# First model of a two-model kernel: conv and rope on VectorE alone, another order of gates, attention and output product

## The chip, the cores and the metric

The kernel runs on one core of a Trainium2 chip. The metric is the device time of one execution in microseconds. Engines are named as in the profile: PE is TensorE's matmul, PEld its weight load, DVE is VectorE, ACT is ScalarE, POOL is GpSimd, SP is SyncE (which here only issues DMAs).

## The reference

Two models of depth 2 run one after the other on 256 tokens of width 1024, all in float32; the change touches only the first. One layer of the first model is, cut to what matters:

```python
n = rmsnorm(h, norm_g[i])
z = n @ w_in[i] + b_in[i]
(c_val, c_glu, c_gate, p_in, p_gate, q, k, v, a_gate, qi, ki, wi) = jnp.split(z, cut, axis=-1)
ya = conv_module(c_val, c_glu, ...) * silu(c_gate)       # 256 channels
yb = pool_mixer(p_in, ...) * silu(p_gate)                # 256 channels
q, k, qi, ki = rope(q), rope(k), rope(qi), rope(ki)
yc = sparse_attention(q, k, v, qi, ki, wi) * silu(a_gate)  # 512 channels
h = h + concatenate([ya, yb, yc], axis=-1) @ w_out[i]
h = h + (p[i] @ ple_w[i]) * sigmoid(h @ ple_gate_w[i])
```

`conv_module` multiplies `val * sigmoid(glu)`, convolves each channel over time with 31 taps (causal, depthwise), then layernorm, silu and a 256 x 256 product. `rope` rotates halves of each head. `sparse_attention` scores all keys with a small indexer (`qi`, `ki`, `wi`), keeps the 64 best per query, and runs softmax attention of 8 heads over those.

## The kernel before

**Layout and tiles.** Activations lie with channels on partitions and the 256 tokens along the free axis. A weight *unit* is 128 x 1024 float32 (512 KB): one output tile of 128 columns with 8 blocks of 128 rows. `rawunit` (L421, its transfer L425) loads it on SP's queue into one of 4 buffers `raw`; `unit` (L431) splits it into a high half `hl[:, 0]` on ACT (L437) and a low half `hl[:, 1]` on DVE (L445), 4 buffers. `mtile` (L542) multiplies one tile: 8 blocks, each three products (`mm3`, L384 to L386: high x high, high x low, low x high) into a PSUM bank `mm`. A few first tiles use the unsplit weights (`ftile`).

**Stages of `layer1` (L716).** In source order: value and glu tiles of the convolution; the key-index tile `ki`, with rope; the token-major tiles `pin` (pooling input and index weights); 2 query-index tiles `qi`, with rope; 4 tiles `q` and 4 tiles `k`, each group with rope; 4 units of `v`; 8 gate tiles `sil`; the output product in two halves of 8 tiles, each over 4 blocks of the concatenation `cat` (`xx[:, 0]`); then the per-layer embedding. `cat` holds convolution in blocks 0 and 1, pooling in 2 and 3, the four head pairs of attention in 4 to 7. The first half of the output product contracts blocks 0 to 3, the second 4 to 7.

**Other work in between.** The convolution (`conv1`), the indexer (`index1`), pooling (`pool1`) and attention (`attn1`) are generators in a list `tasks`. After each tile `tick` (L463) runs tasks with a budget of 1500: it takes the first task that does something, and subtracts the cost that its `yield` names. `add(..., front=True)` puts a task first. With `turns` set, each task that was tried goes to the end of the list. `until` runs tasks up to a named result, `flush` runs all to their end. A task that lacks an input yields `None`. In the first layer the matrix for the second model's modulation is also computed in small pieces (`ada`, `wada` transfers), one piece per tick. The tasks set the source order; the compiler then orders each engine's queue itself, by dependencies and source order, so that an instruction may run well ahead of work written before it.

**The convolution (L927).** For channel block `j` of 2, `acc[:, j]` starts as tap 0 times the input `u` (L931) and takes 30 more taps (`taps`, L934). Those of `j = 0` are one DVE instruction each (`stt`, L392). With `CONV_POOL = 1` those of `j = 1` are all two instructions: ACT scales the input into `zh` (one of 2 buffers, L405), and GpSimd adds it to `acc` (L943). The task of `j = 1` is put first with cost 200 for two taps, the other has 800. Then follow the layernorm, silu, the product `pw` and the gate (from L954 on), which need the value tiles to be done (`late`). The output product begins when `conv` and `pool` are done (L871, L872); all tasks are flushed before its second half.

**Rope (L695).** For two tiles at a time: a shuffle on DVE into `ropes` (L704), two products with cosine and sine (L707, L708) and a sum (L709), each 128 x 512. With `ROPE = 'qk'` the latter three are on GpSimd for `q` and `k`, which makes 12 per layer, and on DVE for `qi` and `ki`.

**Attention (L1051).** Eight steps (4 head pairs x 2 query blocks): two score products, mask and maximum on DVE (`aL`, L1067), exponential on ACT, transposes and value products on PE, then the gate and the split into `cat`. It is put last in the list, behind convolution and pooling, and begins when the masks `imk` are there.

**Order of the gates.** `GATES` names which gate each of the 8 gate tiles is; it also orders weights and biases on the host.

Of the kernel before, what the change touches and what calls it, by code (L numbers as in the profile page):

```python
# [24 lines left out]
DOWN_PACE = 2.5  # L25
CONV_POOL = 1
CONVP = 200
CONVY = 800
INNER = 500
# [20 lines left out]
PINR = True  # L50
ROPE = 'qk'
ROPEB = 2
# [43 lines left out]
def head_cols(base, heads):  # L96
# [4 lines left out]
    0, 256, 512, 768, 1024, 1280, 1792, 2304, 2816, 3328, 3584, 3648)  # L101
GATES = [("c", 0), ("c", 1), ("a", 0), ("p", 0), ("p", 1), ("a", 1), ("a", 2), ("a", 3)]
B1_TILES = (
# [15 lines left out]
def block1_units(i, a):  # L119
    w = a["w_in"][i]  # L120
    u = [fm(w, c) for c in B1_TILES[:5]]
    u += tm(w, TOKC, 3)
    u += [fm(w, c) for c in B1_TILES[5:15]]
    u += tm(w, rng(V, 512), 2)
    u += [fm(w, c) for c in B1_TILES[15:]]
    wo = a["w_out"][i]
    u += [np.concatenate([fm(wo[g * 512 : g * 512 + 512], rng(m * 128, 128)) for m in (m0, m0 + 1)], 1)
          for g in range(2) for m0 in range(0, 8, 2)]
    pw = a["ple_w"][i]
    u += [np.concatenate([fm(pw, rng(m * 128, 128)) for m in range(g * 4, g * 4 + 4)], 1) for g in range(2)]  # L130
    gw = a["ple_gate_w"][i]
    u += [fm(gw, rng(m * 128, 128)) for m in range(8)]
    return u
# [216 lines left out]
class Prog:  # L350
# [191 lines left out]
    def mtile(s, c0, n, unit=None, ks=range(KT), off=0):  # L542
        hl = unit if unit is not None else s.unit()
        ps = s.bank("mm")
        ks = list(ks)
        for k in ks:
            o = (k + off) * 128
            w = [hl[:, e, o : o + 128] for e in range(2)]
# [167 lines left out]
    def layer1(s, i):  # L716
# [104 lines left out]
        for nme in ("q", "k"):  # L821
            raw = s.t([128, 4, T], nme + "r", 1)
            for j in range(4):
                ps = wtile()
                s.a(raw[:, j], ps[:, :T], AF.Identity, bias=bias()[0])
                s.tick()
            s.rope(raw, 4, nc.gpsimd if nme in ROPE else None)
            qk.append(raw)
# [16 lines left out]
        if i == 0:  # L845
            s.pin(nc.scalar.dma_start(s.x2[:, :, :T], A["ctxT"].rearrange("p (k t) -> p k t", k=KT)))
        s.add(s.attn1(qk[0], qk[1], v, cat, st8))
        s.pace = PACE[2]
# [21 lines left out]
        s.pool_share = 0.0  # L870
        s.until(st8, "conv")  # L871
        s.until(st8, "pool")  # L872


        for g in range(2):
            if g:
                s.flush()
            for m in range(KT):
                if m % 2 == 0:
                    hl = s.unit()  # L880
                ps = s.mtile(0, T, hl, range(4 * g, 4 * g + 4), m % 2 * 4 - 4 * g)
                s.tt(h[:, m], h[:, m], ps[:, :T], ALU.add)
                if g:
                    s.split(s.xx[:, 1, 0, m], s.xx[:, 1, 1, m], h[:, m])
                s.tick()
# [41 lines left out]
    def conv1(s, i, P, H, u, cat, st8):  # L927
        nc = s.nc
        acc = s.t([128, 2, T], "acc", 1)
        for j in range(2):  # L930
            s.ts(acc[:, j], u[:, j, 0:T], P["dw"][:, j * CONV_K : j * CONV_K + 1], ALU.mult,  # L931
                 P["dwb"][:, j : j + 1], ALU.add)

        def taps(j, cost):  # L934
            for k in range(1, CONV_K):
                w = P["dw"][:, j * CONV_K + k : j * CONV_K + k + 1]
                x = u[:, j, k : k + T]
                if j == 0 or k < CONV_POOL:
                    s.stt(acc[:, j], x, w, acc[:, j], ALU.mult, ALU.add)
                else:  # L940
                    pr = s.t([128, T], "zh", 2)
                    s.a(pr, x, AF.Copy, scale=w)
                    nc.gpsimd.tensor_tensor(acc[:, j], acc[:, j], pr, ALU.add)  # L943
                if k % 2 == 0:
                    yield cost
            st8["taps", j] = True

        s.add(taps(1, CONVP), front=True)
        yield from taps(0, CONVY)
        while ("taps", 1) not in st8:  # L950
            yield None
        while "late" not in st8:
# [98 lines left out]
    def attn1(s, q, k, v, cat, st8):  # L1051
# [22 lines left out]
        for n, (pr, qt) in enumerate(steps):  # L1074
# [38 lines left out]
            s.tt(yc, po[:, :T], st8["a", pr], ALU.mult)  # L1113
            s.split(cat[0][:, 4 + pr], cat[1][:, 4 + pr], yc)
            yield 700

# [635 lines left out]
```

## Time and profile before

| | |
|---|---|
| median of 3 runs | 1469.65 us (1467.91 to 1471.45) |
| profiled execution | 1469.05 us, its span 1467.2 us |
| instructions | 25799 |
| granted clock, mean | 0.979 of full speed |
| busy: PE | 1403.8 us |
| busy: DVE | 1057.1 us |
| busy: ACT | 695.6 us |
| busy: POOL | 160.3 us |
| moved by DMA | 218.02 MB |

The first model takes the first 430 us or so of the span: its first layer up to about 230 us, its second from there. In a profile's row the engine, line and operation stand first, then the tile written and those read (`out<-in`), shapes, the count, busy time and mean duration. Busy time counts overlapping instructions once; a duration can be longer than the time from one start to the next, since an engine begins an instruction before the record of the one ahead has ended. The granted clock is TensorE's, as a share of 2.4 GHz; its other level is 1.2 GHz, and a share in between is a mean over a stretch.

### The profile page before, as it was taken

The numbers are of one execution on the slowest core, as the hardware profiler recorded it, in microseconds if no ns is written. First come the engines' busy times: TensorE is split into PE (matmuls) and PEld (weight loads), VectorE is DVE, ScalarE is ACT, GpSimd is POOL, SyncE is SP. The second block draws the span as 40 slices with busy tenths as digits, with TensorE's granted clock in tenths as the row PEclk, the third lists the DMA queues.
The fourth block names the chain that finished last, engine by engine and source line by source line (L and its number), as shares of the span: only waits on it lengthen the run. The fifth ranks groups of instructions, "written<-read, shape, count | busy, mean of one in ns | idle before, by whom it ended". The sixth has DMA issues, their size and how long they took to land.

```text
span 1467.2 us, 25799 instructions
## 1 busy us (share of the span) xinstructions
PE 1403.8 (96%) x10178; PEld 1196.6 (82%) x10178; DVE 1057.1 (72%) x2128; ACT 695.6 (47%) x1294; POOL 160.3 (11%) x176
## 2 busy tenths in 40 slices
PE   8889999689999999999999999999999999999997
PEld 7657688677997877768888888888898887999997
DVE  6895656996976655465898886787367665698694
ACT  4635655636765233454444422343246245476562
POOL 1840001920020000002100000000210000100001
PEclk9999999999999999999999999999999999999998
DMA  7677685343452211112353565555333233376662
GB/s 263 249 254 263 206 310 187 101 144 115 135 172 86 88 59 55 58 55 101 89 183 117 164 223 201 171 186 174 89 97 101 87 97 92 108 211 195 185 197 77
DMA packets 63761, 218.02 MB, mean 149 GB/s; under 512 B 7254, under 2 KB 12312, under 8 KB 63512
## 3 DMA queue, kind: packets, MB, share of 16 engines
q1 hardware_dynamic: 58224, 208.17, 44.7%
q10 hardware_dynamic: 5416, 8.20, 1.8%
q8 instruction: 80, 1.31, 0.4%
q14 instruction: 41, 0.34, 0.1%
HBM read 215.30 MB, written 1.05 MB: 147 GB/s over the span
## 4 chain that ended last, share of the span: by engine, by line
PE 79%; DVE 9%; POOL 4%; issue 3%; ACT 3%; DMA 2%; ACTq 0%; POOLq 0%; DVEq 0%; SPq 0%
PE mm L384 21%; PE mm L385 21%; PE mm L386 21%; PE ax L381 10%; DVE hl L445 3%; POOL acc L943 2%; PE mm L381 2%; PE ada L381 2%; DMA raw<-in_units_dram 1%; DVE acc L392 1%; PE ax L1705 1%; ACT hl L437 1%; POOL sqa L526 1%; DVE isc L392 1%; DVE xx L392 1%
## 5 line engine op out<-in xcount | busy, mean ns | idle before, releaser
L384 PE MATMUL mm<-xx,hl 128*128 128x256 f32 (+1 forms) x1720 | 557.9, 326 | 16.2 <-ACT qr L405 7.6
L386 PE MATMUL mm<-xx,hl 128*128 128x256 f32 (+1 forms) x1720 | 549.0, 320 | 4.9 <-DVE hl L445 4.9
L385 PE MATMUL mm<-xx,hl 128*128 128x256 f32 (+1 forms) x1720 | 549.7, 320 | 0.0
L445 DVE TENSOR_TENSOR hl<-raw,hl 128x1024 fp32r<-128x1024 f32 x286 | 359.2, 1256 | 107.4 <-ACT hl L437 104.2
L437 ACT ACTIVATE hl<-raw 128x1024 fp32r<-128x1024 f32 x286 | 301.0, 1054 | 172.9 <-PE mm L386 151.3
L384 PEld LDWEIGHTS mm<-xx,hl 128*128 128x128 f32 x1720 | 328.4, 191 | 60.5 <-issue 13.1
L386 PEld LDWEIGHTS mm<-xx,hl 128*128 128x128 f32 x1720 | 328.7, 191 | 32.2 <-DVE hl L445 6.3
L385 PEld LDWEIGHTS mm<-xx,hl 128*128 128x128 f32 x1720 | 328.9, 192 | 29.7 <-issue 6.3
L392 DVE SCALAR_TENSOR_TENSOR y<-mm,sp,y 128x255 f32<-128x255 f32 (+1 forms) x184 | 109.1, 595 | 25.8 <-ACT y L405 24.3
L384 PE MATMUL mm<-hid,hl 128*128 128x256 f32 (+1 forms) x374 | 123.0, 329 | 0.0
L385 PE MATMUL mm<-hid,hl 128*128 128x256 f32 (+1 forms) x374 | 123.0, 329 | 0.0
L386 PE MATMUL mm<-hid,hl 128*128 128x256 f32 (+1 forms) x374 | 122.7, 328 | 0.0
L405 ACT ACTIVATE y<-mm,sp 128x256 f32<-128x256 f32 (+1 forms) x92 | 60.4, 657 | 116.2 <-PE mm L386 116.0
L526 POOL TENSOR_TENSOR sqa<-sqa,sq 128x256 f32<-128x256 f32 x36 | 32.1, 896 | 690.5 <-ACT sq L405 689.8
L384 PEld LDWEIGHTS mm<-hid,hl 128*128 128x128 f32 x374 | 70.5, 188 | 7.2
L385 PEld LDWEIGHTS mm<-hid,hl 128*128 128x128 f32 x374 | 70.5, 188 | 7.1
L386 PEld LDWEIGHTS mm<-hid,hl 128*128 128x128 f32 x374 | 70.5, 188 | 6.9
L392 DVE SCALAR_TENSOR_TENSOR x<-mm,mod,x 128x256 f32<-128x256 f32 x96 | 43.5, 478 | 44.2 <-PE mm L386 44.0
L385 PE MATMUL mm<-hl,xx 128*128 128x416 f32 (+3 forms) x192 | 68.4, 356 | 5.2 <-DVE hl L445 5.2
L664 DVE CUSTOM_DVE_ANT_0 wada<-wada,crow,sp 128x1024 f32<-128x1024 f32 x48 | 61.0, 1280 | 11.1 <-DMA wada<-in_wadaT_dram 10.8
L384 PE MATMUL mm<-hl,xx 128*128 128x416 f32 (+3 forms) x192 | 68.1, 356 | 0.4 <-DVE glr L1306 0.2
L386 PE MATMUL mm<-hl,xx 128*128 128x416 f32 (+3 forms) x192 | 67.1, 350 | 0.0
(279 smaller groups left out, 1752.1 us busy)
## 6 DMA issues: line engine op xcount, KB each, us to landing
raw<-in_units_dram SPq DMA_DIRECT2D x296, 512.0 KB, 3.7
wada<-in_wada_dram SPq DMA_DIRECT2D x48, 512.0 KB, 4.9
wada<-in_wadaT_dram SPq DMA_DIRECT2D x48, 512.0 KB, 4.6
nab<-in_nab_dram ACTq DMA_DIRECT2D x12, 192.0 KB, 2.5
x<-in_xT_dram SPq DMA_DIRECT2D x4, 256.0 KB, 5.2
x<-in_ctxT_dram ACTq DMA_DIRECT2D x1, 1024.0 KB, 6.6
crow<-in_crow_dram SPq DMA_DIRECT2D x1, 1024.0 KB, 6.6
c<-in_c_dram ACTq DMA_DIRECT2D x1, 928.0 KB, 5.2
```

Source lines behind the costliest of these rows:

```text
L381: return s.nc.tensor.matmul(out, lhsT, rhs, start=start, stop=stop, **kw)
L384: s.nc.tensor.matmul(out, l[0], r[0], start=start, stop=False)
L385: s.nc.tensor.matmul(out, l[0], r[1], start=False, stop=False)
L386: s.nc.tensor.matmul(out, l[1], r[0], start=False, stop=stop)
L392: s.nc.vector.scalar_tensor_tensor(out, a, sc, b, op0, op1)
L405: s.nc.scalar.activation(out, in_, func, bias=bias, scale=scale)
L437: a = nc.scalar.activation(hl[:, 0], raw, AF.Copy)
L445: b = nc.vector.tensor_sub(hl[:, 1], raw, hl[:, 0].bitcast(F32))
L526: (eng or s.nc.vector).tensor_tensor(st["acc"], st["acc"], sq, ALU.add)
L664: nc.vector.tensor_tensor_reduce(out=out, in0=w, in1=c[:, j], scale=1.0, scalar=bias[:, m : m + 1], op0=ALU.mult, op1=ALU.add, accum_out=m ...
L943: nc.gpsimd.tensor_tensor(acc[:, j], acc[:, j], pr, ALU.add)
L1705: nc.tensor.transpose(pt[:, kt * 128 : kt * 128 + 128], L[j][:, kt * 128 : kt * 128 + 128], s.ident)
```

## The change

It touches the first model only, in six places. (1) All 60 convolution taps of a layer are DVE instructions, both channel blocks in turn, with a cost of 900 for each two; no tap is on ACT and GpSimd. (2) All rope work is on DVE. (3) Attention is put first in the task list, and from there up to the second half of the output product the tasks take turns. (4) The gate tiles come in the order pooling 0, attention 0, pooling 1, attention 1 to 3, convolution 0 and 1. (5) The output product contracts blocks 2 to 5 (pooling and the first two head pairs) in its first half and 6, 7, 0, 1 (the other head pairs and the convolution) in its second; the rows of `w_out` are put in that order on the host, and `mtile` counts blocks of the unit by position. (6) The first half waits for pooling and the second head pair, no longer for the convolution, which only the flush before the second half waits for.

```diff
--- before.py
+++ after.py
@@ -23,9 +23,7 @@
 FIRST = 2
 PAIR_PACE = 1.7
 DOWN_PACE = 2.5
-CONV_POOL = 1
-CONVP = 200
-CONVY = 800
+CONVY = 900
 INNER = 500
 INNER_K = (3,)
 R_TICK, NQ_TICK, SC_TICK = 1500, 2500, 3000
@@ -48,7 +46,7 @@
 PRE = 0
 WARM2 = (3, 3, 3)
 PINR = True
-ROPE = 'qk'
+
 ROPEB = 2
 START = (0, 0)
 RAW0 = (0, 2)
@@ -99,7 +97,10 @@
 
 C_VAL, C_GLU, C_GATE, P_IN, P_GATE, Q, K, V, A_GATE, QI, KI, WI = (
     0, 256, 512, 768, 1024, 1280, 1792, 2304, 2816, 3328, 3584, 3648)
-GATES = [("c", 0), ("c", 1), ("a", 0), ("p", 0), ("p", 1), ("a", 1), ("a", 2), ("a", 3)]
+GATES = [("p", 0), ("a", 0), ("p", 1), ("a", 1), ("a", 2), ("a", 3), ("c", 0), ("c", 1)]
+
+
+WO_ORDER = (2, 3, 4, 5, 6, 7, 0, 1)
 B1_TILES = (
     [rng(C_VAL, 128), rng(C_VAL + 128, 128), rng(C_GLU, 128), rng(C_GLU + 128, 128)]
     + [head_cols(KI, [0]) + head_cols(KI, [0])]
@@ -123,7 +124,7 @@
     u += [fm(w, c) for c in B1_TILES[5:15]]
     u += tm(w, rng(V, 512), 2)
     u += [fm(w, c) for c in B1_TILES[15:]]
-    wo = a["w_out"][i]
+    wo = np.concatenate([a["w_out"][i][k * 128 : k * 128 + 128] for k in WO_ORDER])
     u += [np.concatenate([fm(wo[g * 512 : g * 512 + 512], rng(m * 128, 128)) for m in (m0, m0 + 1)], 1)
           for g in range(2) for m0 in range(0, 8, 2)]
     pw = a["ple_w"][i]
@@ -543,8 +544,8 @@
         hl = unit if unit is not None else s.unit()
         ps = s.bank("mm")
         ks = list(ks)
-        for k in ks:
-            o = (k + off) * 128
+        for q, k in enumerate(ks):
+            o = (q + off) * 128
             w = [hl[:, e, o : o + 128] for e in range(2)]
             s.mm3(ps[:, :n], w, [s.mv(e, k, c0, n) for e in range(2)], k == ks[0], k == ks[-1])
             if s.inner and k in INNER_K:
@@ -824,7 +825,7 @@
                 ps = wtile()
                 s.a(raw[:, j], ps[:, :T], AF.Identity, bias=bias()[0])
                 s.tick()
-            s.rope(raw, 4, nc.gpsimd if nme in ROPE else None)
+            s.rope(raw, 4)
             qk.append(raw)
 
         s.pool_share = SHARE[1]
@@ -844,7 +845,8 @@
         st8["late"] = True
         if i == 0:
             s.pin(nc.scalar.dma_start(s.x2[:, :, :T], A["ctxT"].rearrange("p (k t) -> p k t", k=KT)))
-        s.add(s.attn1(qk[0], qk[1], v, cat, st8))
+        s.add(s.attn1(qk[0], qk[1], v, cat, st8), front=True)
+        s.turns = True
         s.pace = PACE[2]
         sil = s.t([128, 8, T], "sil", 1)
         if i == DEPTH - 1:
@@ -868,17 +870,18 @@
             s.tick()
         s.pace = PACE[3]
         s.pool_share = 0.0
-        s.until(st8, "conv")
         s.until(st8, "pool")
+        s.until(st8, ("att", 1))
 
 
         for g in range(2):
             if g:
+                s.turns = False
                 s.flush()
             for m in range(KT):
                 if m % 2 == 0:
                     hl = s.unit()
-                ps = s.mtile(0, T, hl, range(4 * g, 4 * g + 4), m % 2 * 4 - 4 * g)
+                ps = s.mtile(0, T, hl, WO_ORDER[4 * g : 4 * g + 4], m % 2 * 4)
                 s.tt(h[:, m], h[:, m], ps[:, :T], ALU.add)
                 if g:
                     s.split(s.xx[:, 1, 0, m], s.xx[:, 1, 1, m], h[:, m])
@@ -930,25 +933,11 @@
         for j in range(2):
             s.ts(acc[:, j], u[:, j, 0:T], P["dw"][:, j * CONV_K : j * CONV_K + 1], ALU.mult,
                  P["dwb"][:, j : j + 1], ALU.add)
-
-        def taps(j, cost):
-            for k in range(1, CONV_K):
-                w = P["dw"][:, j * CONV_K + k : j * CONV_K + k + 1]
-                x = u[:, j, k : k + T]
-                if j == 0 or k < CONV_POOL:
-                    s.stt(acc[:, j], x, w, acc[:, j], ALU.mult, ALU.add)
-                else:
-                    pr = s.t([128, T], "zh", 2)
-                    s.a(pr, x, AF.Copy, scale=w)
-                    nc.gpsimd.tensor_tensor(acc[:, j], acc[:, j], pr, ALU.add)
-                if k % 2 == 0:
-                    yield cost
-            st8["taps", j] = True
-
-        s.add(taps(1, CONVP), front=True)
-        yield from taps(0, CONVY)
-        while ("taps", 1) not in st8:
-            yield None
+        for k in range(1, CONV_K):
+            for j in range(2):
+                s.stt(acc[:, j], u[:, j, k : k + T], P["dw"][:, j * CONV_K + k : j * CONV_K + k + 1], acc[:, j],
+                      ALU.mult, ALU.add)
+            yield CONVY
         while "late" not in st8:
             yield None
         o256 = s.t([128, 128], "o256", 1)
@@ -1112,6 +1101,7 @@
             yc = s.t([128, T], "yc", 2)
             s.tt(yc, po[:, :T], st8["a", pr], ALU.mult)
             s.split(cat[0][:, 4 + pr], cat[1][:, 4 + pr], yc)
+            st8["att", pr] = True
             yield 700
```

## Rows read from the trace of the kernel before

**Rows 1.** Head of the page.

```profile
span 1467.2 us, 25799 instructions
```

**Rows 2.** Windows: width; busy PE, PEld, DVE, ACT, POOL (count); clock, DMA, GB/s.

```profile
24.00:107.00 83.00, 68.98 (x497) 54.88 (x496) 77.09 (x140) 43.64 (x78) 50.26 (x43) 0.94 0.74 254
107.00:195.00 88.00, 86.54 (x746) 65.41 (x747) 54.28 (x142) 46.16 (x106) 0.82 (x1) 1.00 0.74 249
244.00:322.00 78.00, 60.95 (x410) 55.38 (x409) 74.01 (x127) 41.16 (x72) 48.81 (x42) 0.91 0.45 138
322.00:391.00 69.00, 68.22 (x533) 58.70 (x532) 55.71 (x144) 46.17 (x107) 1.59 (x2) 1.00 0.40 124
730.00:780.00 50.00, 50.00 (x216) 40.36 (x215) 47.06 (x70) 20.07 (x28) 0.00 (x0) 1.00 0.54 165
```

**Rows 3.** Waits of PE, 24 to 107 us: total us, times, longest.

```profile
PE ada L381 <- ACT adae L405: 5.3, 1, 5.3
PE mm L386 <- DVE hl L445: 4.9, 5, 2.1
```

**Rows 4.** Waits of PE, 244 to 322 us.

```profile
PE mm L384 <- ACT qr L405: 7.6, 3, 4.4
PE mm L385 <- DVE hl L445: 4.0, 1, 4.0
```

**Rows 5.** DVE groups, 24 to 107 us: busy us, mean ns | idle before.

```profile
L445 DVE TENSOR_TENSOR hl<-raw,hl 128x1024 fp32r<-128x1024 f32 x19 | 27.2, 1438 | 4.7 <-ACT hl L437 4.7
L392 DVE SCALAR_TENSOR_TENSOR acc<-u,sp,acc 128x256 f32<-128x256 f32 x30 | 23.9, 797 | 0.5
...
L392 DVE SCALAR_TENSOR_TENSOR isc<-irl,pin,isc 128x256 f32<-128x256 f32 x3 | 2.2, 740 | 0.0
L1041 DVE MAX8 im<-iwk 128x8 f32<-128x128 f32 x7 | 2.0, 279 | 0.0
...
L707 DVE TENSOR_TENSOR qi<-qi,c 128x512 f32<-128x512 f32 x1 | 1.2, 1242 | 0.0
```

**Rows 6.** DVE groups, 244 to 322 us.

```profile
L445 DVE TENSOR_TENSOR hl<-raw,hl 128x1024 fp32r<-128x1024 f32 x19 | 28.3, 1489 | 2.2 <-ACT hl L437 2.2
L392 DVE SCALAR_TENSOR_TENSOR acc<-u,sp,acc 128x256 f32<-128x256 f32 x28 | 23.4, 835 | 0.2
```

**Rows 7.** DVE groups, 322 to 391 us.

```profile
L445 DVE TENSOR_TENSOR hl<-raw,hl 128x1024 fp32r<-128x1024 f32 x17 | 20.7, 1217 | 0.1
...
L392 DVE SCALAR_TENSOR_TENSOR acc<-u,sp,acc 128x256 f32<-128x256 f32 x2 | 1.0, 478 | 0.0
...
L401 DVE TENSOR_TENSOR v<-mm,tokb 128x512 f32<-128x512 f32 x1 | 0.7, 669 | 0.0
```

**Rows 8.** POOL groups, 24 to 107 us.

```profile
L943 POOL TENSOR_TENSOR acc<-acc,zh 128x256 f32<-128x256 f32 x30 | 30.4, 1012 | 18.9 <-ACT zh L405 17.0
L708 POOL TENSOR_TENSOR ropes<-ropes,c 128x512 f32<-128x512 f32 x4 | 7.5, 1864 | 0.0
```

**Rows 9.** An ACT group, 24 to 107 us.

```profile
L405 ACT ACTIVATE zh<-u,sp 128x256 f32<-128x256 f32 x30 | 14.8, 505 | 14.2 <-POOL acc L943 14.2
```

**Rows 10.** Tile acc, first layer: ns min/median/max, first and last start us.

```profile
L392 DVE SCALAR_TENSOR_TENSOR acc<-u,sp,acc x30: 459/835/1518, 26.8 to 89.6; 128x256 f32<-128x256 f32 x30
```

**Rows 11.** DVE in order of time, first layer: start us, duration us.

```profile
81.36 0.47 DVE L392 SCALAR_TENSOR_TENSOR acc<-u,sp,acc 128x256 f32<-128x256 f32 x1
81.75 0.28 DVE L1041 MAX8 im<-iwk 128x8 f32<-128x128 f32 x1
...
105.58 0.29 DVE L398 TENSOR_SCALAR imk<-imk 128x256 f32<-128x256 f32 x1
```

**Rows 12.** DVE in order of time, second layer.

```profile
327.46 0.48 DVE L392 SCALAR_TENSOR_TENSOR acc<-u,sp,acc 128x256 f32<-128x256 f32 x1
...
344.88 0.43 DVE L411 TENSOR_TENSOR xx<-acc,xx 128x256 fp32r<-128x256 f32 x1 [0.36 <-ACT xx L410]
```

**Rows 13.** Tile aL, both layers: first and last start us.

```profile
L1067 DVE CUSTOM_DVE_ANT_0 aL<-ax,imk x32: 270/348/425, 145.0 to 371.8; 128x128 f32<-128x128 f32 x16, 128x256 f32<-128x256 f32 x16
```

## The prediction

> **What bounds the kernel now.** I read the page's head, then busy times by stretch, then the waits of PE, then VectorE (DVE) group by group. The profiled execution spans 1467.2 us [rows 1] and took 1469.05 us, 0.6 us under the median of the three runs, 1469.65; I make the sum on 1469.05 and add the 0.6. PE carries the kernel, but not evenly [rows 2]. In 24 to 107 us (first layer, from the key-index tile to the value tiles) it is busy 68.98 of 83 us at a clock of 0.94, and in 244 to 322 us (the same part of the second layer) 60.95 of 78 us at 0.91. In the stretches behind each (gates, attention, output product) it idles 1.5 and 0.8 us at full clock. So this change can win at most what is lost in two stretches, which I call A and B. In A that is 14.0 us idle and 68.98 x 0.06 = 4.1 us of clock: floor 64.8 us. In B it is 17.1 us and 60.95 x 0.09 = 5.5 us: floor 55.5 us.
>
> What PE waits for there is named in [rows 3, 4]: the low halves of weights (`hl` on DVE, 4.9 us in A, 4.0 in B), the copy `adae` (5.3 us) and the copies `qr` (7.6 us), both on ACT. The reader should look one step further back. DVE is busy 77.09 of 83 us in A and 74.01 of 78 in B [rows 2], so it is the engine behind `hl`. ACT is not full (43.64 us), but its queue is in order, and 30 scaled copies `zh` for GpSimd's convolution taps stand in it and sat 14.2 us waiting for GpSimd [rows 9]; what is queued behind them, `hl` high halves and the copies that free PE's banks, waits with them.
>
> Now the point on which all rests. DVE's 77 us are not 77 us of work. In A the same instruction costs more than behind B, where GpSimd does nearly nothing: a tap 797 ns against 478, a low half 1438 against 1217, an index sum 740 against a tap's 478, a rope product of 512 columns 1242 against 669 for the addition of that width [rows 5, 7]. MAX8, with one input, takes 279 ns between them [rows 5]. GpSimd's own taps take 1012 ns and its rope products 1864 [rows 8]. So GpSimd and DVE delay each other where both take two tensors from SBUF, and A and B are where GpSimd works (50.26 and 48.81 us, [rows 2]).
>
> **The change, part by part.**
>
> *Taken away on GpSimd.* 30 taps and 12 rope products per layer [rows 8]. GpSimd's time costs nothing by itself; what goes with it is DVE's stretching. A: 19 x (1.438 - 1.217) + 30 x (0.797 - 0.478) + 3 x (0.740 - 0.478) + 3 x (1.242 - 0.669) = 4.2 + 9.6 + 0.8 + 1.7 = 16.3 us [rows 5, 7]. B: 19 x (1.489 - 1.217) + 28 x (0.835 - 0.478) and the same 2.5 = 17.7 us [rows 6, 7].
>
> *Taken away on ACT.* 30 `zh` copies per layer, 14.8 us of busy time and the 14.2 us of waiting in A [rows 9]. I count no sum of its own for it: it is a part of the PE idle above, and ACT then has over half the stretch free.
>
> *Added on DVE.* 30 taps per layer. From start to start a tap takes 81.75 - 81.36 = 0.39 us [rows 11], since the next begins before the end that the record shows; 30 x 0.39 = 11.7 us. 12 rope products of 512 columns: nearest row 0.669 us [rows 7], less the same overlap of 0.09 gives 0.58; 7.0 us. Together 18.7 us per layer. With whole durations it is 14.3 + 8.0 = 22.3; I take the lower, the one that adjacent starts show, and keep the other for a rival.
>
> All in place, DVE needs 77.1 - 16.3 + 18.7 = 79.5 us in A and 74.0 - 17.7 + 18.7 + 0.8 (two taps that lie past 322) = 75.8 in B. That is what it needs now. So the change gains nothing by mere exchange; it gains if work leaves A and B.
>
> *What can leave.* The 60 taps of a layer, 23.4 us. Without them DVE needs 56.1 us in A and 52.4 in B, close to PE's floors. Today the convolution must be ready for the first half of the output product; after the change only for the second half, behind attention. The queues are not in source order: the first layer's DVE taps run from 26.8 to 89.6 us, spread between other work [rows 10], though most are written behind the query tiles. Taps fill gaps, and what does not fit goes on in the next stretch. I put A at 70 us and B at 62 us, 5.2 and 6.5 above the floors, about 40% of today's idle time. The choice lies nearest the row at 730 to 780 us, where DVE is busy 47.06 of 50 us and PE has no gap [rows 2]; I stay above it because B has almost no DVE slack. At 70 us A holds (70 - 56.1) / 0.39 = 35 taps; 25 go on into 107 to 195 us, 9.8 us on top of 54.28 of 88: free. At 62 us B holds 24; 36 go on, 14.0 us less the 0.8 that are there now, on top of 55.71 of 69: 68.9 of 69, full. I charge 4 us.
>
> *Order.* Attention now stands first in the task list and shares turns. Today the masks end at 105.58 us [rows 11], yet the first score is read at 145.0 [rows 13], since convolution and pooling are issued first. PE idles 1.5 us in that stretch, so an earlier start is worth 0 to 2.3 us in both layers; I take 0. The new wait, second head pair before the first half, holds the 96 matrix products of that half on PE. Attention has some 30 us of gate tiles to finish four steps in; I count 0. If it is late, the first half is.
>
> *Gates and output weights.* The same tiles, the same 512 KB units, other columns and rows: no instruction or transfer more on SP's queue, and none moved past another. 0. DMA stays under PE: A's share of 0.74 of 83 us is 61.4 us of full rate [rows 2], below 70.
>
> Sum: -13 - 16 + 4 = -25. 1469.05 - 25 + 0.6 = 1444.6 us.
>
> **Against a rule.** The rows say that GpSimd's help costs DVE 16 to 18 us where it saves 18.7. The Trainium skill (Perfetto Trace Analysis, Optimizing Scalar/DVE Operations) says that with a saturated DVE, handing work to ScalarE or even GpSimd may make sense, and adds that between DVE and GpSimd a shared read port may spoil it. Its first half speaks against this change; by it the sum would be that of the last rival.
>
> **The rivals.**
>
> 1. *The convolution's tail stands open.* In B the last tap starts at 327.46 us and the low half of its result ends at 344.88 + 0.43, 17.9 us later [rows 12], today under gate tiles. If DVE is full up to the end of the output product's first half, the second half waits for that chain. In A DVE has room for the taps, so I charge B alone: 1444.6 + 17.9 = 1462.5. For it: B's 68.9 of 69. Against: taps stand ahead of later attention steps.
>
> 2. *Taps come too early (slower).* If the 60 taps are all placed ahead of the last value unit, as today's 30 were in A, DVE keeps its work and its idle time of 5.9 and 4.0 us: A 85.4 (+2.4), B 79.8 (+1.8), 1473.9; with whole durations 7 more. It decides from (83 - 5.9 - 56.1) / 0.39 = 54 taps in A, 55 in B. For it: early taps in [rows 10]. Against: without the stretching other work comes ready sooner and leaves fewer gaps.
>
> 3. *The long rows are not GpSimd's doing.* Then the change only adds 18.7 us per layer to a full DVE: 1469.65 + 37.4 = 1507. Against it: MAX8 stays at 279 ns in the same stretch [rows 5], and behind B the prices fall.
>
> **How the numbers follow.** Forecast 0.74, tail 0.13, early taps 0.10, last rival 0.03. What a measurement here can tell from no change is about 0.2%, 3 us. Faster: 0.74 and most of the tail, 0.85. Same: what lies between, a lighter early fill or a tail in both layers, 0.05. Slower: 0.10. Low end: both floors, -18.2 - 22.5, and 2.3 for attention: 1426.7. High end: past the tail's 1462.5, to 1466; early taps and the last rival stay outside.
>
> **What would show it.** Right: taps near 480 ns and low halves near 1.22 us in A and B, GpSimd nearly idle, no `zh` copies with a tap scale, A about 70 and B about 62 us, clock there nearer 1, taps running on into the gates. The tail shows as a PE gap before the ninth output tile; early taps as over 54 taps before the value addition and DVE full at the old length. Wrong at the root: taps still near 800 ns with GpSimd idle. Also wrong: PE waiting in A and B for DMA, or for the first half's attention tiles.

## The result and the profile after

| | before | after |
|---|---|---|
| median of 4 runs, us | 1470.55 (1467.91 to 1474.62) | 1454.57 (1449.16 to 1459.26) |
| profiled execution, us | 1469.05 | 1459.26 |
| its span, us | 1467.2 | 1457.5 |
| its granted clock | 0.979 | 0.975 |

The ratio is 0.9888, with a 95% interval of 0.9846 to 0.9929: 16 us faster. The profiled execution of after is the slowest of its four, so the place of the time is read from the trace and its sum from the medians. Two instructions mark the stages, in both traces: V, the start of the second value addition (`v<-mm` on DVE), and E, the start of the last `th<-th,ple` product on DVE, near the end of a layer.

| stretch, us | before | after | difference | forecast |
|---|---|---|---|---|
| start to V, layer 1 (holds A) | 107.5 | 87.6 | -19.9 | -13 |
| V to E, layer 1 | 118.1 | 126.7 | +8.6 | 0 |
| E to V, layer 2 (holds B) | 96.1 | 73.7 | -22.4 | -16 |
| V to E, layer 2 | 95.4 | 112.7 | +17.3 | +4 |
| rest: second model, same code | 1050.1 | 1056.8 | +6.7 | 0 |

The first model ends 16.4 us earlier, near the 16.0 between the medians. The last line is no effect of the change: over the profiled executions of all kernels of this document it lies between 1045.3 and 1057.0 us, in no order that follows their edits.

V and E are marks on DVE, and they do not cut PE's work at the same place in both kernels: between V and E of the first layer PE runs 288 products of `ada` in after and 252 in before; in the stretch behind it none in after and some 30 in before. PE's lost time depends less on that. It is the length of a stretch less PE's busy time times the granted clock, here rounded to whole us.

| PE, us | before: busy, clock | lost | after: busy, clock | lost |
|---|---|---|---|---|
| start to V, layer 1 | 90.0, 0.95 | 22 | 81.8, 1.00 | 6 |
| V to E, layer 1 | 117.1, 1.00 | 1 | 124.0, 0.99 | 4 |
| E to V, layer 2 | 79.2, 0.93 | 23 | 71.9, 0.98 | 3 |
| V to E, layer 2 | 94.5, 1.00 | 1 | 103.1, 0.92 | 18 |

So 36 us are won in the stretches that hold A and B, and 20 are given back behind them, nearly all of it in the second layer. Of the 8.6 us that the first layer's V to E is longer, some 5 are work of PE that lies there now.

The head of the page of after, beside [rows 1]:

```profile
span 1457.5 us, 25654 instructions
...
PE 1411.3 (97%) x10178; PEld 1203.0 (83%) x10178; DVE 1053.6 (72%) x2212; ACT 669.9 (46%) x1234; POOL 63.1 (4%) x92
```

GpSimd (POOL) is down from the 160.3 us of before to 63.1. The windows of after (width; busy PE, PEld, DVE, ACT, POOL with counts; clock, DMA share, GB/s), which answer to [rows 2]. Lines of the code have moved: 384 of before is 385 here.

```profile
24.00:88.00 64.00, 61.17 (x480) 50.11 (x479) 62.95 (x148) 29.77 (x46) 0.00 (x0) 1.00 0.94 330
...
232.00:288.00 56.00, 54.53 (x377) 48.73 (x377) 54.71 (x134) 25.55 (x39) 0.00 (x0) 0.97 0.52 166
288.00:373.00 85.00, 75.56 (x543) 65.71 (x543) 69.02 (x171) 46.66 (x105) 3.21 (x2) 0.90 0.37 114
```

In A, PE is busy 61.17 of 64 us at a clock of 1.00 where it was 68.98 of 83 at 0.94; in B, 54.53 of 56 at 0.97. GpSimd does nothing there. But the stretch behind B, which had PE without a gap, is now 85 us long with PE busy 75.56 at 0.90. DVE's groups in A, beside [rows 5]:

```profile
L446 DVE TENSOR_TENSOR hl<-raw,hl 128x1024 fp32r<-128x1024 f32 x19 | 23.0, 1215 | 0.2 <-ACT hl L438 0.2
L393 DVE SCALAR_TENSOR_TENSOR acc<-u,sp,acc 128x256 f32<-128x256 f32 x24 | 10.5, 478 | 0.0
L709 DVE TENSOR_TENSOR ropes<-ropes,c 128x512 f32<-128x512 f32 x5 | 3.4, 685 | 0.0
...
L1030 DVE MAX8 im<-iwk 128x8 f32<-128x128 f32 x7 | 2.0, 285 | 0.0
...
L393 DVE SCALAR_TENSOR_TENSOR isc<-irl,pin,isc 128x256 f32<-128x256 f32 x3 | 1.4, 471 | 0.0
```

Low halves of weights went from 1438 to 1215 ns, taps from 797 to 478, index sums from 740 to 471; MAX8 stays (279, now 285). PE's waits in A (total, times, longest), beside [rows 3]:

```profile
PE mm L385 <- ACT hl L438: 1.7, 2, 1.4
PE mm L386 <- DVE hl L446: 1.2, 1, 1.2
```

The waits for `adae` are gone, and 2.9 us are left. Tile `acc` in the first layer (ns min/median/max, first and last start), beside [rows 10]: the last tap starts at 127.5 us, 37.9 later than before. 24 taps of the first layer start ahead of V, and 20 of the second.

```profile
L393 DVE SCALAR_TENSOR_TENSOR acc<-u,sp,acc x60: 464/478/497, 26.8 to 127.5; 128x256 f32<-128x256 f32 x60
```

What was gained there is partly lost between the two halves of the output product. From the last tile of the first half to the first of the second passed 3.5 and 4.8 us before (173.98 to 177.47, 376.18 to 380.94); now it is 18.1 and 20.1 us. These two pauses by their windows:

```profile
154.00:172.00 18.00, 16.23 (x134) 10.12 (x127) 7.80 (x24) 5.89 (x11) 0.70 (x1) 0.91 0.74 252
342.00:362.00 20.00, 12.90 (x57) 9.81 (x56) 12.24 (x25) 5.34 (x10) 1.60 (x1) 0.70 0.34 105
```

The first costs PE less, since pieces of `ada` fill it: 18 - 16.23 x 0.91 = 3.2 us lost. In the second, PE is busy 12.90 us at a clock of 0.70, a mean between its two levels: by the same estimate 20 - 12.90 x 0.70 = 11.0 us lost. What DVE does in it, in order of time (start, duration; in brackets the idle time ahead and what ended it):

```profile
341.84 0.42 DVE L402 TENSOR_TENSOR x<-x,mm 128x256 f32<-128x256 f32 x1 [0.53 <-PE mm L387]
342.18 1.27 DVE L393 SCALAR_TENSOR_TENSOR acc<-u,sp,acc 128x256 f32<-128x256 f32 x3
...
350.47 0.75 DVE L402 TENSOR_TENSOR acc<-acc,ax 128x256 f32<-128x256 f32 x2 [1.94 <-PE ax L382]
...
355.72 0.48 DVE L393 SCALAR_TENSOR_TENSOR acc<-ax,sp,sil 128x256 f32<-128x256 f32 x1 [1.86 <-PE ax L382]
...
358.61 0.42 DVE L402 TENSOR_TENSOR yc<-ax,sil 128x256 f32<-128x256 f32 x1
...
361.90 0.42 DVE L402 TENSOR_TENSOR x<-x,mm 128x256 f32<-128x256 f32 x1 [1.93 <-PE mm L387]
```

and PE:

```profile
343.11 1.13 PE L382 MATMUL ax<-acc,o 128*128 128x256 f32 x4 [0.28 <-DVE acc L393]
...
345.96 1.25 PE L382 MATMUL ax<-c,csq 128*128 128x1 f32 x8 [0.82 <-ACT csq L406]
...
349.14 1.22 PE L382 MATMUL ax<-c,clr 128*128 128x128 f32 x4 [1.51 <-POOL clr L509]
352.75 3.78 PE L382 MATMUL ax<-csq,sw 128*128 128x256 f32 x8 [2.38 <-DVE csq L393]
...
357.91 0.66 PE L382 MATMUL ax<-aPT,v 128*64 128x128 f32 x8 [0.69 <-ACT aPT L406]
359.54 0.62 PE L385 MATMUL mm<-xx,hl 128*128 128x256 f32 x3 [0.98 <-ACT xx L411]
```

Only behind the last tile of the first half (341.84) do the last three taps run; then comes the whole tail of the convolution, mean (343.11), variance (345.96), normalisation (349.14), its product (352.75) and result (355.72), and behind it the value product of the fourth head pair (357.91, gate at 358.61). Then the second half starts.

### The profile page after: what moved, and what is told of

It is laid out like the page before. It is cut to its first block, busy times and chain, and to the rows that moved or that the text cites. A ratio compares the mean times of both kernels' runs of the same rounds, so it can differ in the third digit from the quotient of the medians.

```text
span 1457.5 us, 25654 instructions
## 1 busy us (share of the span) xinstructions
PE 1411.3 (97%) x10178; PEld 1203.0 (83%) x10178; DVE 1053.6 (72%) x2212; ACT 669.9 (46%) x1234; POOL 63.1 (4%) x92
## 4 chain that ended last, share of the span: by engine, by line
PE 80%; DVE 8%; issue 6%; ACT 3%; DMA 2%; POOL 1%; ACTq 0%; POOLq 0%; DVEq 0%
PE mm L385 22%; PE mm L386 21%; PE mm L387 21%; PE ax L382 10%; DVE hl L446 2%; PE ada L382 2%; PE mm L382 1%; PE ax L1695 1%; DMA raw<-in_units_dram 1%; DMA wada<-in_wada_dram 1%; POOL sqa L527 1%; ACT hl L438 1%; DVE xx L393 1%; DVE nf L393 1%; ACT slA L408 1%
## 5 line engine op out<-in xcount | busy, mean ns | idle before, releaser
L446 DVE TENSOR_TENSOR hl<-raw,hl 128x1024 fp32r<-128x1024 f32 x286 | 349.5, 1222 | 99.4 <-ACT hl L438 97.5
L393 DVE SCALAR_TENSOR_TENSOR y<-mm,sp,y 128x255 f32<-128x255 f32 (+1 forms) x184 | 109.1, 595 | 27.6 <-ACT y L406 25.9
L386 PE MATMUL mm<-hl,xx 128*128 128x416 f32 (+3 forms) x192 | 67.0, 351 | 2.5 <-DVE hl L446 2.5
L385 PE MATMUL mm<-hl,xx 128*128 128x416 f32 (+3 forms) x192 | 66.2, 349 | 0.4 <-DVE glr L1296 0.2
L387 PE MATMUL mm<-hl,xx 128*128 128x416 f32 (+3 forms) x192 | 66.2, 346 | 0.0
```

Of the source, the lines that this page charges most:

```text
L385: s.nc.tensor.matmul(out, l[0], r[0], start=start, stop=False)
L386: s.nc.tensor.matmul(out, l[0], r[1], start=False, stop=False)
L387: s.nc.tensor.matmul(out, l[1], r[0], start=False, stop=stop)
L393: s.nc.vector.scalar_tensor_tensor(out, a, sc, b, op0, op1)
L446: b = nc.vector.tensor_sub(hl[:, 1], raw, hl[:, 0].bitcast(F32))
```

## The experiments

Every ratio is to runs of before taken beside it, with its 95% interval. The table gives, for each profiled execution, the convolution taps that DVE starts ahead of V in the first and second layer, of how many; the four stretches named above in us; and the two pauses between the halves of the output product.

| kernel | taps ahead | to V | V to E | E to V | V to E | pauses |
|---|---|---|---|---|---|---|
| before | 30 / 28 of 30 | 107.5 | 118.1 | 96.1 | 95.4 | 3.5 / 4.8 |
| after | 24 / 20 of 60 | 87.6 | 126.7 | 73.7 | 112.7 | 18.1 / 20.1 |
| dve_only | 42 / 40 of 60 | 97.1 | 122.3 | 84.7 | 107.1 | 3.4 / 6.3 |
| order_only | 30 / 26 of 30 | 107.4 | 119.9 | 92.5 | 97.6 | 2.2 / 2.2 |
| convy300 | 48 / 48 of 60 | 94.3 | 119.0 | 85.0 | 97.9 | 2.3 / 2.2 |
| few_taps | 10 / 10 of 10 | 88.5 | 117.5 | 73.6 | 94.2 | 2.3 / 2.2 |
| late300 | 24 / 20 of 60 | 89.8 | 120.2 | 72.9 | 100.9 | 6.6 / 5.2 |
| late100 | 25 / 20 of 60 | 86.5 | 119.6 | 72.8 | 101.6 | 2.2 / 5.2 |
| no_tail | 24 / 20 of 60 | 89.5 | 125.8 | 73.6 | 111.8 | 18.2 / 19.7 |
| attn_first | 24 / 20 of 60 | 90.0 | 124.6 | 73.8 | 105.8 | 16.9 / 17.0 |
| taps_gpsimd | 21 / 13 of 30 | 102.2 | 122.5 | 86.7 | 96.6 | 2.2 / 2.2 |
| rope_gpsimd | 41 / 27 of 60 | 97.1 | 128.8 | 80.1 | 104.4 | 18.5 / 16.1 |
| rope_gpsimd_hold | 40 / 26 of 60 | 99.1 | 125.7 | 83.5 | 103.4 | 19.3 / 16.1 |
| few_taps_rope_gpsimd | 10 / 10 of 10 | 90.8 | 115.7 | 81.3 | 91.8 | 2.3 / 2.2 |

**dve_only: the engines' part alone.** On before:

```diff
-CONV_POOL = 1
+CONV_POOL = 31
-ROPE = 'qk'
+ROPE = ''
```

> The kernel before with all taps and all rope on VectorE and nothing else changed (order of gates, tasks and output product as before). Theory (GpSimd's work stretched VectorE's; the gain is made in the two stretches from the key-index tile to the value tiles, and given back behind them): taps near 0.48 us, the value addition of the first layer at 85 to 92 us instead of 107.5, that of the second 25 to 40 us earlier, GpSimd idle there; as the convolution is still asked for first, its tail lies under the gate tiles; 15 to 30 us below the kernel before. Rival (the order of attention and output product makes the gain, the exchange of engines none, since VectorE needs as much time as before): within 4 us of the kernel before.

1466.96 us, 0.9957 [0.9929, 0.9985]. The stages that hold A and B are 10.4 and 11.4 us shorter, about half of what after gains there, with 42 and 40 taps ahead. Behind V the stretches are 4.2 and 11.7 us longer. In the first layer PE is busy throughout (122.06 of 122.4 us), so that is work that lies there now; in the second it loses some 11 us, and what causes that was not followed. A's window up to V:

```profile
24.00:97.00 73.00, 65.67 (x487) 52.33 (x486) 68.41 (x165) 30.17 (x46) 0.00 (x0) 0.98 0.84 301
```

GpSimd does nothing there, yet DVE is busy 68.41 of 73 us. Both expectations missed: the part alone is worth 5.6 us.

**order_only: the order alone.** On after, taps of block 1 back on ACT and GpSimd as in before, and for `q` and `k`:

```diff
+CONV_POOL = 1
+CONVP = 200
...
-            s.rope(raw, 4)
+            s.rope(raw, 4, nc.gpsimd)
```

> The changed kernel with the taps of the second channel block back on ScalarE and GpSimd and the rope of q and k back on GpSimd; gates, turns and output product as changed. Theory: taps near 0.8 us, both stretches as long as before (value additions near 107 and 320 us), total within 5 us of the kernel before, or over it if the convolution's tail stands open. Rival (the order makes the gain): 10 to 16 us below the kernel before.

1472.37 us, 1.0003 [0.9971, 1.0036]; the first model ends within 0.3 us of before. DVE's groups, 24 to 100 us:

```profile
L395 DVE SCALAR_TENSOR_TENSOR acc<-u,sp,acc 128x256 f32<-128x256 f32 x30 | 23.9, 796 | 0.5
L448 DVE TENSOR_TENSOR hl<-raw,hl 128x1024 fp32r<-128x1024 f32 x16 | 23.5, 1474 | 4.7 <-ACT hl L440 4.7
```

The stretching is there as in [rows 5], the value additions are at 107.4 and 319.8 us, and all came as expected: the order alone gives nothing. So -5.6 and 0 apart are -16 together. But a third thing differs between these two and after, the cost of the taps' turns: in both, the taps of block 1 still come first with a cost of 200 for two, where after has 900 for each two. That cost, and not the order, sets how many taps stand ahead of V, as the next run shows; what the order adds at the cost of after (dve_only with that cost) was not run.

**convy300, few_taps: how many taps stand where.** On after, one line each.

```diff
-CONVY = 900
+CONVY = 300
```

> The changed kernel with a cost of 300 instead of 900 for each two taps, so that the taps stand earlier in the source, and the convolution's layernorm and product with them. Theory (what was won in the two stretches is given back because the convolution's tail is issued last): the pause between the last tile of the output product's first half and the first of its second half, 18.1 us in the first layer and 20.1 in the second, falls under 8 us each, and the total to 1438 to 1450. Rival (PE would have been as late anyhow, since VectorE or attention sets the end of these stretches): pause shorter, but the total stays at 1450 to 1458.

1449.8 us, 0.9856 [0.9817, 0.9896]. 48 taps are ahead in both layers, and the stages are 6.7 and 11.3 us longer than in after; 28 taps more in B by 0.39 us are 10.9. But both pauses are closed, as expected, and the first model ends 4.6 us earlier than in after. The median is 4.8 us lower, which is within the intervals of the two, and it lies on the border between theory and rival.

```diff
-        for k in range(1, CONV_K):
+        for k in range(1, 6):
```

> The changed kernel with 5 instead of 30 further taps for each channel block, which leaves 50 of 60 VectorE taps of a layer out, about 19.5 us of VectorE time per layer. Theory: VectorE's load behind the two stretches is what pushes the convolution's tail out; without it the pause before the second half falls under 10 us in both layers, and the total to 1425 to 1442. Rival (the tail is late by its place in the source, not by VectorE's load): the pause stays over 12 us, and the total falls by less than 8 us.

1431.36 us, 0.9725 [0.9685, 0.9765]. Time and pauses came as the theory had them, but leaving taps out takes their turns away as well as their load on DVE, so this run does not tell the two apart; the next two do. With 10 taps ahead the stages are no shorter than with the 24 and 20 of after (88.5 and 73.6 against 87.6 and 73.7): there PE is the bound. With more taps ahead DVE is nearly full: by the prediction's sum dve_only needs 56.1 + 0.39 x 42 = 72.5 us, where A took 97.1 - 24 = 73.1 (DVE busy 68.41). With the 48 of convy300 the sum gives 74.8, 4.5 more than the 70.3 that A took (DVE busy 68.98), so it is too high there.

**late300, late100: a smaller cost only behind the value tiles.** On after (late100 has 100):

```diff
-            yield CONVY
+            yield CONVY if "late" not in st8 else 300
```

> The changed kernel with a cost of 900 for two taps up to the value tiles and of 300 behind them. Theory (few taps ahead of the value addition and an early tail are both worth having, and the changed kernel has the first, the one with 300 throughout the second): 20 to 28 taps ahead of the value addition in each layer, the pause before the second half under 8 us in both layers, total 1436 to 1446. Rival (taps issued in a rush behind the value tiles displace attention on VectorE, so that the first half starts later by what the pause gave): total 1448 to 1456.

1437.32 us, 0.9812 [0.978, 0.9844]. As many taps ahead as in after, and the pauses are down to 6.6 and 5.2 us: taps, pauses and time as expected.

> As with 900 up to the value tiles and 300 behind them, with 100 behind them: the whole convolution stands in the source right behind the value tiles. Theory (the earlier the convolution's chain, the shorter the pause before the second half): pause under 5 us in both layers, total 1430 to 1438. Rival (at this cost the taps displace attention on VectorE and the first half starts later): first half's first tile 5 us or more later than with 300 (131 and 322 us), total 1440 or more.

1436.03 us, 0.9766 [0.9742, 0.979]: the time as expected, the second pause 0.2 us over the 5 that were. Its windows, and DVE where the halves meet in the second layer:

```profile
24.00:87.00 63.00, 60.73 (x476) 49.66 (x475) 61.74 (x144) 29.79 (x46) 0.00 (x0) 1.00 0.93 331
87.00:172.00 85.00, 84.22 (x738) 64.11 (x737) 66.09 (x176) 45.83 (x105) 0.85 (x2) 1.00 0.73 244
225.00:279.00 54.00, 52.94 (x385) 48.38 (x383) 53.42 (x131) 25.24 (x39) 0.00 (x0) 1.00 0.55 180
279.00:352.00 73.00, 69.49 (x546) 60.70 (x545) 68.22 (x173) 45.96 (x104) 1.56 (x2) 1.00 0.43 131
```

```profile
338.11 0.41 DVE L402 TENSOR_TENSOR x<-x,mm 128x256 f32<-128x256 f32 x1
...
339.57 1.06 DVE L393 SCALAR_TENSOR_TENSOR acc<-ax,sp,sil 128x256 f32<-128x256 f32 x2
...
343.36 1.30 DVE L402 TENSOR_TENSOR x<-x,mm 128x256 f32<-128x256 f32 x3
```

The convolution's result (339.57) falls into the end of the first half. The second layer's stretch behind B is 73 us at a clock of 1.00, against 85 at 0.90 in after. With A and B left as they are, closing the pauses is worth 17.3 us (late300) and 18.5 (late100) between the medians, 16.8 and 20.2 at the end of the first model, and the cost of a turn sets it: the DVE work is the same as in after. late100 is the fastest that has all its taps, 34 us under before.

**no_tail: the second half does not wait for the convolution.** On after; the second half reads pooling's blocks in the convolution's place.

```diff
-            s.mm3(ps[:, :n], w, [s.mv(e, k, c0, n) for e in range(2)], k == ks[0], k == ks[-1])
+            s.mm3(ps[:, :n], w, [s.mv(e, k + 2 if s.skip and k < 2 else k, c0, n) for e in range(2)], k == ks[0], k == ks[-1])
...
                 s.turns = False
                 s.flush()
+                s.skip = True
```

> The changed kernel, whose second half of the output product reads pooling's two blocks again in place of the convolution's: the same instructions and the same VectorE load, but the second half does not wait for the convolution, whose part is left out of the result. Theory (that wait is what gives back the gain): pause before the second half under 6 us in both layers, total 8 to 16 us below the changed kernel, 1438 to 1447. Rival (PE has only moved its filling work, the pieces for the second model's modulation, and loses nothing in the first layer; in the second the wait goes over to the fourth head pair): less than 5 us below the changed kernel.

1445.93 us, 0.9851 [0.9828, 0.9875], but both pauses are there, and the second layer's E is at 400.73 us, where after has 400.72: the first model gained nothing in this execution. Where the 8.6 us between the medians come from is not shown; the second model of this execution is the shortest of all (1045.3 us). DVE across the pause:

```profile
342.39 0.42 DVE L403 TENSOR_TENSOR x<-x,mm 128x256 f32<-128x256 f32 x1 [0.51 <-PE mm L388]
...
356.94 0.48 DVE L394 SCALAR_TENSOR_TENSOR acc<-ax,sp,sil 128x256 f32<-128x256 f32 x1 [0.37 <-PE ax L383]
...
359.14 0.42 DVE L403 TENSOR_TENSOR yc<-ax,sil 128x256 f32<-128x256 f32 x1
...
362.13 0.42 DVE L403 TENSOR_TENSOR x<-x,mm 128x256 f32<-128x256 f32 x1 [0.44 <-PE mm L388]
```

The gate of the fourth head pair is at 359.14, behind the convolution's tail, and 3.0 us later the second half's first tile is added. My theory that taking away the wait for the convolution closes the pause missed: what comes last is attention, which stands behind the convolution's tail. In the second layer that is the rival's account; its total, less than 5 us below after, was not met either.

**attn_first: attention ahead in the flush.** On after, ahead of `s.flush()`:

```diff
+                s.tasks.sort(key=lambda g: g.__name__ != "attn1")
```

> The changed kernel; in the flush before the second half attention's rest is issued ahead of the convolution's. Without the wait for the convolution the pause stayed, so something else holds the second half: the fourth head pair, whose product is read at 169.4 and 358.6 us, right at the pause's end. Theory (the flush issues the convolution's chain first, and attention's last step stands behind it in the in-order queues): the fourth pair is done 8 us or more earlier in both layers, the pause shrinks by 4 us or more, total 1442 to 1452. Rival (the convolution's chain then stands behind attention and holds the second half itself): the pair is earlier, the pause as long or longer, total 1453 to 1462.

1443.5 us, 0.9827 [0.9782, 0.9873]. DVE across the second layer's pause:

```profile
339.94 0.42 DVE L402 TENSOR_TENSOR x<-x,mm 128x256 f32<-128x256 f32 x1 [0.51 <-PE mm L387]
...
342.60 0.42 DVE L402 TENSOR_TENSOR yc<-ax,sil 128x256 f32<-128x256 f32 x1
...
354.27 0.48 DVE L393 SCALAR_TENSOR_TENSOR acc<-ax,sp,sil 128x256 f32<-128x256 f32 x1 [1.92 <-PE ax L382]
354.91 0.48 DVE L393 SCALAR_TENSOR_TENSOR acc<-ax,sp,sil 128x256 f32<-128x256 f32 x1 [0.15 <-PE ax L382]
...
356.94 0.84 DVE L402 TENSOR_TENSOR x<-x,mm 128x256 f32<-128x256 f32 x2
```

The fourth pair's gate is now at 342.60, 16.0 us earlier, and the pause is still 17.0 us: now the convolution's result at 354.27 is the last. In the first layer the gate comes 11.5 us earlier and the pause is 16.9 us. So there are two waits in succession, and either alone holds the second half. The total, 11 us under after, is what the theory had, but the pauses are only 1.2 and 3.0 us shorter, where it had 4 or more: in the second layer's pause the clock is 0.80 where after has 0.70, and behind it 1.00 where after has 0.92, and the first model ends 6.5 us earlier.

**taps_gpsimd, rope_gpsimd, few_taps_rope_gpsimd: parts of the work back on GpSimd.** On after: the taps of block 1 as in order_only; the rope of `q` and `k`; that same rope with few_taps.

> The changed kernel with the taps of the second channel block back on ScalarE and GpSimd, rope on VectorE. Theory: the taps are the larger part of GpSimd's work (30.4 of 50 us in the first layer), so most of the gain goes: value additions near 100 us and 310 us, total 1462 to 1474. Rival (ScalarE's and GpSimd's help with 30 taps is worth its price once the rope is away, since VectorE has less to do): 1448 to 1458.

1458.63 us, 0.994 [0.9916, 0.9964]. The stages are 14.6 and 13.0 us longer than in after with fewer taps on DVE, at 680 ns in the mean from 24 to 100 us; the pauses are closed, and the stretches behind V are 4.2 and 16.1 us shorter. The value additions (102.2 and 311.4 us) are where the theory had them; the total lies between theory and rival, 0.6 us above the rival's range.

> The changed kernel with the rope products of q and k back on GpSimd, taps on VectorE. Theory (any two-input work on GpSimd beside VectorE's stretches both): rope products 1.2 to 1.9 us each on GpSimd, some taps and low halves over 0.8 and 1.5 us, the value additions 3 to 8 us later than in the changed kernel, total 1457 to 1465. Rival (12 products are too few to hurt, and they spare VectorE 7 us per layer): within 3 us of the changed kernel or below it.

1467.07 us, 0.9985 [0.9964, 1.0005]. It loses 12.5 of the 16 us, more than expected. DVE's groups from 24 to 100 us, and one of GpSimd's from 24 to 107:

```profile
L446 DVE TENSOR_TENSOR hl<-raw,hl 128x1024 fp32r<-128x1024 f32 x20 | 26.0, 1304 | 0.6 <-ACT hl L438 0.6
L393 DVE SCALAR_TENSOR_TENSOR acc<-u,sp,acc 128x256 f32<-128x256 f32 x41 | 25.5, 651 | 0.0
```

```profile
L709 POOL TENSOR_TENSOR ropes<-ropes,c 128x512 f32<-128x512 f32 x4 | 6.7, 1678 | 0.0
```

12 products on GpSimd, 17.2 us of its work, come with a mean tap of 651 ns in A. The trace tells the taps apart: the 9 that overlap a GpSimd product in time average 1289 ns, the other 32 take 471; of the low halves 2 overlap, 2134 ns against 1212. That is some 9 us of stretching. And 41 taps are ahead in the first layer, where after has 24: DVE is free where rope was, and taps move in, 17 x 0.39 = 6.6 us for the 7.0 that rope left. V comes 9.5 us later, so in this layer the stretching is, by this estimate, nearly all of it.

> The kernel with 5 further taps for each channel block (50 of 60 taps of a layer left out), and rope of q and k on GpSimd again; to be held against the run with few taps and rope on VectorE (1431.4 us, value additions at 88.5 us and 279.6 us). The run that was to keep the taps out of the stretch did not do so: 40 of them were still issued ahead of the first value addition, so this one leaves them out. Theory (rope on GpSimd costs by the taps that move into its place on VectorE, and by their stretching): without taps GpSimd's rope costs nothing or gains, total 1426 to 1435, value addition at 84 to 90 us. Rival (12 rope products on GpSimd stretch the low halves and index sums, and are late themselves): value addition 4 us or more later than with rope on VectorE, total 1437 or more.

1433.48 us, 0.9746 [0.9709, 0.9783], 2 us above few_taps, within the intervals of the two and inside the theory's range; the value addition, 90.8 us, is 0.8 past it. In the profiled executions the first layer ends 0.5 us later than that of few_taps and the second model starts 5.8 later; with all taps the same rope cost 11.6 and 9.7 against after. So in the first layer the loss needs the many taps, which are there to be stretched; in the second, rope on GpSimd costs without them too, in this one execution.

**rope_gpsimd_hold: the same with the taps held until the value tiles.**

```diff
+        while "late" not in st8:
+            yield None
```

> Rope of q and k on GpSimd as in the run before, but no tap is issued in the source until the value tiles are through. Rope on GpSimd alone cost nearly the whole gain, with 41 taps ahead of the first value addition instead of 24. Theory (the loss came from taps that moved into the place that rope left, each stretched): without them the value addition stands at 85 to 92 us and, in the second layer, 55 to 60 us after the stretch's start, and the total is 1444 to 1458. Rival (12 rope products on GpSimd stretch VectorE's and are late themselves, whatever the taps do): value addition at 95 us or later, total 1460 or more.

1468.75 us, 0.9987 [0.9966, 1.0009]. The hold took no effect on the queue: 40 and 26 taps still run ahead of V, pulled forward from behind the value tiles of the source. The values are the rival's, but the run decides nothing between the two, since the taps did not stay away.

## Why the prediction was right, and where it was off

**What bounds.** Right. In A and B DVE delayed PE, and GpSimd was what made DVE slow: without it low halves, taps and index sums fall to the prices of [rows 7], as each step had it. The run dve_only shows it apart from the order, and the trace of before shows it tap by tap: of the 30 taps in A the 21 that overlap a GpSimd instruction average 936 ns, the 9 others 472 (in B 21 at 959, 7 at 464).

**Added work.** 0.39 us a tap holds: pairs of taps in the trace of after last 0.87 to 0.88 us, 0.48 plus 0.39. Rope products of 512 columns take 685 ns, near the row taken for them (669).

**A at 70 and B at 62 us.** Too cautious. By the marks A took 87.6 - 24 = 63.6 us, B some 55 (73.7, less the 18.4 us that lay before from E to 244 us), both at their floors. The 5.2 and 6.5 us that I added to the floors "because B has almost no DVE slack" were not needed: 24 and 20 taps were held, not 35 and 24, and so DVE's need came down to PE's (62.95 and 61.17 us busy of 64). Between the marks that is 13.3 us more gain than forecast, in lost time some 7. What held so few taps is the cost of 900, which the prediction did not use for it: at 300, 48 stayed.

**The step that failed: "I charge 4 us".** I priced the taps that leave B as DVE time alone. What they cost beside it is the place of what follows them, which the sum put at nothing. With a cost of 900 for each two, and turns shared with attention and pooling, the tasks do not reach the convolution's end before the first half of the output product is written; its tail is written in the flush, ahead of attention's last step, and the second half needs both. Measured between the marks: 8.6 us in the first layer and 17.3 in the second, 25.9 instead of 4; in lost time 3 and 17, about 20. late300 and late100 show it, since they change only that cost behind the value tiles: in late100 PE loses 1 and 4 us in the two stretches, as against 1 and 1 in before. The 3 us that remain are near the 4 charged; the wait was the term that was missing.

**The first rival, the tail standing open,** is what happened, in both layers, not in B alone. That DVE has room in A was true (last tap at 127.5 us), but the tail's first product came only at 154.8: not the last tap held it but its place in the queues. Its price, 17.9 us, is near the 17.3 that the second layer gave back; that is chance, since the pause there was held by two waits and not by this chain alone. Its condition, DVE full up to the end of the first half, was not met: DVE was busy 47.78 of 54 us from 288 to 342. And it lacked the second wait, the fourth head pair, which attn_first and no_tail show.

So the total came out near by two errors that partly cancel, which is luck: -13.3 in the stages and +21.9 behind them, on -25, gives the -16.4 that the first model shows (in lost time about -7 and +16). The mechanism in A and B was right; the give-back was mis-sized by a factor of five to six.

**The other rivals.** Early taps needed 54 ahead of V; 24 and 20 were. That the long rows were not GpSimd's fell by [rows 5] against their rows of after. The Trainium skill (Perfetto Trace Analysis, Optimizing Scalar/DVE Operations) says both that handing work of a full DVE to GpSimd may make sense and that a read port which the two share may spoil it; here the second agrees with the trace (tap 936 ns beside GpSimd in A, 472 without) and the first does not: with that help order_only is where before was, and without it after is 16 us lower.

**What stays open.** Whether the fourth head pair stands behind the convolution's tail by the order of a queue or by a PSUM bank that they share was not tried. late100's V to E in the second layer is still 6.2 us longer than that of before (101.6 against 95.4). Some 3 of these are lost by PE, the rest is work that lies there now; DVE is busy 68.22 of 73 us there, but what ends the last waits was not followed. That few_taps, with 10 taps, loses under 1 us there speaks for the taps' load. Nor is it shown how much of the gain the order makes apart from the taps' cost.

## What to carry to other kernels

Before handing work to a second engine to relieve a full one, compare the full engine's own durations with and without the other at work; the help can cost what it saves. Work moved out of a full stage is not only time for the engine that takes it: follow the chain behind its last instruction to the one that needs its result, and price that chain as open unless something stands over it. Where tasks share turns by costs written by hand, try two settings: here a high cost while the bound stage ran and a low one as soon as it was past was worth some 18 us over the one high cost throughout.

## What the runs showed of the hardware beyond what was expected

Twelve GpSimd products, less than a quarter of a stage's time (17.2 us of 73, to V in rope_gpsimd), already bring the mean tap there from 478 to 651 ns; I had taken the 30 taps for the main burden. The mean hides two prices: a tap that overlaps a 512-column product of GpSimd averages 1289 ns, one that overlaps none 471. Beside GpSimd's 256-column additions alone (taps_gpsimd, 24 to 102 us) it is 782 and 476. And the second layer's pause of after cost PE more than its idle time: 7.1 us idle came with a granted clock of 0.70 over the 20 us, by estimate 3.9 us more, and the clock is still 0.92 in the 11 us behind it, while in the first layer's, where the `ada` pieces kept PE busy 16.23 of 18 us, the clock was 0.91.
